# The delta rule of a hybrid trunk: its steps placed by counts of projection matmuls, decays loaded through GpSimd's queue, two buffers for the decayed products

## The chip, the cores and the metric

The kernel runs on one core of a Trainium2 chip. The metric is device time in microseconds (us) of one execution, as the median of three runs. TensorE multiplies (PE in the profile; PEld is its weight load), VectorE (DVE) and ScalarE (ACT) work element by element and empty the accumulation banks, GpSimd (POOL) masks and can issue transfers, SyncE (SP) issues transfers.

## The reference

Two layers, 1024 tokens, width 1024. In each layer one projection of the normalised input gives the inputs of two branches: attention over selected keys, and a gated delta rule with 8 heads of 128 channels. The sum of the two branches, each with its gate, goes through an output projection and is added to the residual. The change concerns the delta rule:

```python
qkv_b = jax.nn.silu(causal_depthwise_conv(qkv_b, conv_w[layer]))
q_b = l2_normalize(q_b...); k_b = l2_normalize(k_b...)
beta = jax.nn.sigmoid(beta_l); g = -jnp.exp(a_log) * jax.nn.softplus(a_l + dt_bias)
# S_t = a_t (I - b_t k_t k_t^T) S_{t-1} + b_t k_t v_t^T,  o_t = S_t^T q_t,  a_t = exp(g_t)
o_b = chunked_gated_delta_rule(q_b, k_b, v_b, beta, g)
y_b = rms_norm(o_b, gdn_norm_gain) * jax.nn.silu(z_b)
```

The chunked form needs, for each head and chunk, the products k·k and q·k times a matrix of decays, the inverse of a unit triangular matrix, and then a loop over the chunks that carries the state.

## The kernel before, in words

Numbers are float32; the large projections split each operand into a high and a low part and add three float32r matmuls (line 361 for the projections whose output has channels on the partitions). The delta rule uses chunks of 128 tokens, 8 per head.

`feature_phase` (L639) runs once per layer and holds all of the delta rule. Per head, `gdn_front` (L672) projects keys, queries and values (`proj_feat`, L354: two halves of 512 tokens, 24 matmuls each), evacuates them on ScalarE (L687, L688), convolves on VectorE (L694) and applies silu (L696, L697). It then transposes keys and queries on TensorE (L708), squares and adds them on ScalarE (L723, 16 squares of 128 columns, each with a read of its sum), scales kdec and vb from the transposes on VectorE (L713), turns the norms into coefficients (L727 to L737), sends one row of them through memory (L739 to L747), multiplies keys with keys and queries (L758) and multiplies the products with the decays H (L760, L761). `inverse_blocks` (L829) takes the diagonal 32x32 blocks of H through memory into the tile "wide", inverts them in 31 pairs of VectorE operations over 8 rows each (L847, L849), and reads them back through memory (16 reads, L855). `inverse_pairs` (L858) joins blocks in two levels with small matmuls (L871 to L892). `gdn_chunks` (L766) walks the chunks: r from the state (L780, L782), u (L784, copied on VectorE, L786), the next state (L789, L794), the output in two matmuls into two halves of a bank (L797, L798) that VectorE combines (L802, L803), and a square on ScalarE (L806). `gdn_finish` (L810) computes the two gate projections of a head, the norm (L817 to L821), transposes the output (L825), multiplies (L826) and writes it out.

`decay_rows` (L660) loads one head's decays, spread to all partitions, on SP's queue, masks them on GpSimd (L666) and exponentiates them on ScalarE (L669); it runs one head ahead, with three buffers H.

In program order a head's front comes before the previous head's finish, and its chunks behind that. The order on each engine is made by the framework's scheduler: it takes what its own model of time says is ready, by program order, and `high_priority(offset=AHEAD)` puts the block inverses first. Each engine then keeps that order on the chip. The accumulators are two banks "acc" and one "more", in turn; transposes and products share two banks "tr"; the chunk loop has two banks "ch" and one "oc".

Of the kernel before, what the change touches and what calls it, by code (L numbers as in the profile page):

```python
# [25 lines left out]
F32 = mybir.dt.float32  # L26
# [4 lines left out]
AF = mybir.ActivationFunctionType  # L31
# [5 lines left out]
P = 128  # L37
# [31 lines left out]
AHEAD, BEHIND = 1000, -10  # L69
# [17 lines left out]
class Trunk:  # L87
    def __init__(self, ctx, tc, args):
# [10 lines left out]
        self.beside = None  # L99
        ctx.enter_context(self.banks(acc=(1, 2), tr=(1, 2)))  # L100
# [49 lines left out]
    def constants(self, first):  # L150
# [25 lines left out]
        for q in range(4):  # L176
            nc.gpsimd.affine_select(self.xinit[32 * q:32 * q + 32], self.xinit[32 * q:32 * q + 32],
                                    pattern=[[1, 8], [-1, 32]], compare_op=OP.not_equal, fill=1.0, base=8 * q,
                                    channel_multiplier=0)
# [113 lines left out]


# [59 lines left out]
    def proj_feat(self, ws, half, act, evac, tag="acc"):  # L354
# [3 lines left out]
        for k in range(KT):  # L358
            cs = slice((k % 4) * P, (k % 4 + 1) * P)
            for i, (a, b) in enumerate(((0, 0), (0, 1), (1, 0))):  # L360
                self.nc.tensor.matmul(acc, ws[k // 4][a][:, cs], act[b][:, k, hs], start=k == 0 and i == 0,  # L361
                                      stop=k == KT - 1 and i == 2)
        evac(hs, acc)
        self.tick()
# [48 lines left out]
    def decays(self, l, p, raw):  # L413
# [41 lines left out]
        row = p.tile([64, P], F32, name="row")  # L455
        nc.vector.tensor_copy(row, pr[:64, :P])
        self.rows = self.dram.tile([T, 8, P], F32, name="rows")
        nc.sync.dma_start(out=self.rows.rearrange("t h c -> (t h) c"), in_=row)
# [159 lines left out]
    def gated(self, l, ht, cz, cg, tag="acc"):  # L618
# [4 lines left out]
        for half in range(2):  # L623
            b = p.tile([P, 512], F32, name="gate", bufs=2)
            for i in range(2):
                def evac(hs, acc):
                    th = p.tile([P, 512], F32, name="th", bufs=2)
                    nc.scalar.activation(th, acc, AF.Tanh, scale=0.5)
# [10 lines left out]
    def feature_phase(self, l, ht):  # L639
        nc, tc = self.nc, self.tc  # L640
        self.yb = self.dram.tile([HEADS, P, S], F32, name="yb")
        with tc.tile_pool(name="feat", bufs=1) as p, self.banks(ch=(1, 2), oc=(1, 1), more=(1, 1)):
            XF = p.tile([P, T, 64], F32, name="xf")
            nc.gpsimd.memset(XF, 0.0)
            heads = {}
            E = self.decay_rows(p, 0)
            for h in range(HEADS + 1):
                if h < HEADS:
                    H, E = E, self.decay_rows(p, h + 1) if h + 1 < HEADS else None
                    heads[h] = self.gdn_front(l, p, ht, h, H)  # L650
# [4 lines left out]
                if h:  # L655
                    self.gdn_finish(l, p, ht, heads.pop(h - 1))
                if h < HEADS:
                    self.gdn_chunks(p, heads[h], XF)

    def decay_rows(self, p, h):  # L660


        nc = self.nc
        E = p.tile([P, T, P], F32, name="H", bufs=3)
        nc.sync.dma_start(out=E, in_=ap(self.rows, h * P, [[0, P], [8 * P, T], [1, P]]))
        nc.gpsimd.affine_select(E, E, pattern=[[0, T], [1, P]], compare_op=OP.is_ge, fill=MASKED, base=0,  # L666
                                channel_multiplier=-1)
        for c in range(T):
            nc.scalar.activation(E[:, c], E[:, c], AF.Exp, bias=self.ngm[:, c, h:h + 1])  # L669
        return E  # L670

    def gdn_front(self, l, p, ht, h, H):  # L672
        nc = self.nc
        w = self.w_in[l]
        feat = self.feat[l]
        kf = p.tile([P, S], F32, name="kf", bufs=3)
        qf = p.tile([P, S], F32, name="qf", bufs=3)
        vv = p.tile([P, S], F32, name="vv", bufs=1)
        for base, dst in ((1024, kf), (0, qf), (2048, vv)):
            ct = (base + h * P) // P  # L680
            cw = lambda j: feat[:, 24 * j + ct:24 * j + ct + 1]
            xp = p.tile([P, S + 4], F32, name="xp", bufs=2)
            nc.gpsimd.memset(xp[:, 0:4], 0.0)

            def evac(hs, acc):
                o = hs.start
                nc.scalar.copy(xp[:, 4 + o:516 + o], acc)  # L687
                nc.scalar.activation(dst[:, hs], acc, AF.Copy, scale=cw(3))  # L688

            ws = self.feat_weights(w, C_QKVB + base + h * P)  # L690
            for half in range(2):
                self.proj_feat(ws, half, ht, evac)
            for j in range(3):
                nc.vector.scalar_tensor_tensor(dst, xp[:, 1 + j:1 + j + S], cw(j), dst, op0=OP.mult, op1=OP.add)  # L694
            th = xp[:, 4:4 + S]
            nc.scalar.activation(th, dst, AF.Tanh, scale=0.5)  # L696
            nc.vector.scalar_tensor_tensor(dst, th, 1.0, dst, op0=OP.add, op1=OP.mult)  # L697

        sm = self.small
        beta, egc, egs = (a[:, :, h] for a in (self.beta, self.egc, self.egs))  # L700
        kdec = p.tile([P, T, P], F32, name="kdec", bufs=2)
        vb = p.tile([P, T, P], F32, name="vb", bufs=2)

        def turn(src, half):
            pt = self.tr()
            for i in range(4):
                c = 4 * half + i
                nc.tensor.transpose(pt[:, i * P:(i + 1) * P], src[:, c * P:(c + 1) * P], self.ident)  # L708
            return pt

        def scaled(dst, pt, col, half):
            cs = slice(4 * half, 4 * half + 4)
            nc.vector.tensor_mul(dst[:, cs], pt.rearrange("p (c d) -> p c d", c=4),  # L713
                                 col[:, cs, None].to_broadcast([P, 4, P]))
# [431 lines left out]
```

## Time and profile before

| | |
|---|---|
| median of 3 runs | 2727.01 us (2726.43 to 2728.11) |
| the profiled execution | 2725.06 us, span 2723.3 us |
| TensorE busy | 2570.7 us, 94% |
| VectorE, ScalarE, GpSimd busy | 1972.8, 1316.8, 111.9 us |
| mean granted TensorE clock | 0.976 of full speed |
| feature phase, layer 0 | 358.0 to 1096.9 us |
| feature phase, layer 1 | 1702.5 to 2452.0 us |

All numbers of one profile belong to one execution. Busy time counts an instruction from its start to its end, and matmuls overlap, so a busy TensorE is not one at its peak. The granted clock is a share of full speed: 1.0 is 2.4 GHz and 0.5 is 1.2 GHz, and a value between is a mean over the stretch. The phases' bounds are the first matmul of the first head's keys and the end of the last output transposes.

### The profile page before, as it was taken

How to read it: one execution, taken by the hardware profiler on the slowest of the kernel's cores; microseconds unless marked ns; L12 is line 12 of the kernel's file. 1: busy time of each engine (PE TensorE's matmuls, PEld its weight loads, DVE VectorE, ACT ScalarE, POOL GpSimd, SP SyncE). 2: the span in 40 equal slices, each digit the busy share in tenths (PEclk: the TensorE clock that was granted, in tenths of full speed). 3: DMA queues.
4: the chain of work that ended last, by engine and by line, in shares of the span. 5: the costliest groups of instructions: out<-in, count | busy, mean ns of one | idle time of the engine just before them, and what ended most of it. 6: DMA issues, size and time to landing. Idle time of an engine off the chain costs nothing.

```text
span 2723.3 us, 42939 instructions
## 1 busy us (share of the span) xinstructions
PE 2570.7 (94%) x14854; PEld 2140.5 (79%) x14854; DVE 1972.8 (72%) x5450; ACT 1316.8 (48%) x3169; POOL 111.9 (4%) x398
## 2 busy tenths in 40 slices
PE   7999989999999999999999999898999999999998
PEld 7677778777777888898786777686887778888986
DVE  6677967767787775697366888677676777757965
ACT  5579643343333332697245894433333343227962
POOL 0122000000000000000001210000000000000000
PEclk9999999999999999999999999998899999999999
DMA  3113332222222221531420232321212221226324
GB/s 121 48 66 90 85 87 56 49 51 57 61 51 53 50 73 51 174 105 35 157 65 30 78 101 71 77 63 47 53 42 65 51 57 46 69 63 180 92 68 143
DMA packets 283262, 202.95 MB, mean 75 GB/s; under 512 B 55906, under 2 KB 241188, under 8 KB 283044
## 3 DMA queue, kind: packets, MB, share of 16 engines
q1 hardware_dynamic: 283044, 200.20, 26.2%
q8 instruction: 117, 1.92, 0.3%
q14 instruction: 101, 0.83, 0.1%
HBM read 153.80 MB, written 46.33 MB: 73 GB/s over the span
## 4 chain that ended last, share of the span: by engine, by line
PE 68%; DVE 13%; ACT 7%; DMA 6%; issue 5%; POOL 1%; SPq 0%; DVEq 0%; POOLq 0%; ACTq 0%
PE acc L361 20%; PE acc L338 11%; PE more L361 9%; PE acc L1038 4%; PE wide L1006 4%; PE tr L758 2%; PE tr L1029 2%; ACT t_junk L562 2%; PE out L338 2%; ACT g_junk L723 2%; DMA w_raw<-in_w_in_dram 2%; DVE t_junk L544 2%; DVE w_lo L140 2%; DMA H<-rows 2%; PE tr L708 1%
## 5 line engine op out<-in xcount | busy, mean ns | idle before, releaser
L361 PE MATMUL acc<-hi_t,w_hi 128*128 128x512 f32 x1240 | 502.2, 405 | 8.3 <-DVE gate L629 7.3
L361 PE MATMUL acc<-hi_t,w_lo 128*128 128x512 f32 x1240 | 501.9, 405 | 0.0
L361 PE MATMUL acc<-lo_t,w_hi 128*128 128x512 f32 x1240 | 499.6, 403 | 0.0
L139 ACT CAST w_hi<-w_raw 128x512 fp32r<-128x512 f32 (+1 forms) x336 | 201.1, 602 | 371.0 <-PE acc L361 196.8
L140 DVE TENSOR_TENSOR w_lo<-w_raw,w_hi 128x512 fp32r<-128x512 f32 (+1 forms) x336 | 223.3, 668 | 149.2 <-ACT w_hi L139 136.0
L338 PE MATMUL acc<-w_hi,hi_t 128*128 128x512 f32 (+1 forms) x768 | 285.7, 373 | 12.6 <-ACT w_hi L139 7.3
L338 PE MATMUL acc<-w_lo,hi_t 128*128 128x512 f32 (+1 forms) x768 | 284.5, 371 | 2.1 <-DVE w_lo L140 1.9
L338 PE MATMUL acc<-w_hi,lo_t 128*128 128x512 f32 (+1 forms) x768 | 283.6, 369 | 0.0
L361 PEld LDWEIGHTS acc<-hi_t,w_hi 128*128 128x128 f32 x1240 | 236.7, 191 | 49.8 <-DVE gate L629 8.6
L361 PEld LDWEIGHTS acc<-hi_t,w_lo 128*128 128x128 f32 x1240 | 236.2, 190 | 41.1
L361 PEld LDWEIGHTS acc<-lo_t,w_hi 128*128 128x128 f32 x1240 | 236.3, 191 | 40.9
L562 ACT ACTIVATE t_junk<-scores,t_bits 128x640 f16<-128x640 f32 x248 | 198.8, 802 | 30.8 <-DVE t_bits L554 26.0
L361 PE MATMUL more<-hi_t,w_hi 128*128 128x512 f32 x488 | 198.8, 407 | 4.5 <-ACT kf L688 4.5
L361 PE MATMUL more<-hi_t,w_lo 128*128 128x512 f32 x488 | 199.2, 408 | 0.0
L361 PE MATMUL more<-lo_t,w_hi 128*128 128x512 f32 x488 | 198.3, 406 | 0.0
L338 PEld LDWEIGHTS acc<-w_hi,hi_t 128*128 128x128 f32 x768 | 146.2, 191 | 40.6 <-ACT w_hi L139 10.5
L338 PEld LDWEIGHTS acc<-w_lo,hi_t 128*128 128x128 f32 x768 | 146.7, 191 | 27.4 <-DVE w_lo L140 5.1
L338 PEld LDWEIGHTS acc<-w_hi,lo_t 128*128 128x128 f32 x768 | 146.6, 191 | 22.0 <-issue 1.0
L544 DVE TENSOR_SCALAR_CACHE_REDUCE t_junk<-scores,t_bits 128x1024 f16<-128x1024 f32 (+4 forms) x136 | 153.4, 1128 | 4.3
L849 DVE TENSOR_TENSOR xc<-xc,xtmp 128x248 f32<-128x248 f32 (+30 forms) x496 | 141.8, 286 | 3.1
L847 DVE TENSOR_TENSOR xtmp<-wide,xc 128x248 f32<-128x248 f32 (+30 forms) x496 | 141.6, 285 | 2.7
L806 ACT ACTIVATE o_junk<-vb 128x128 f32<-128x128 f32 x128 | 39.6, 310 | 162.3 <-DVE vb L803 126.3
(344 smaller groups left out, 5478.4 us busy)
## 6 DMA issues: line engine op xcount, KB each, us to landing
w_raw<-in_w_in_dram SPq DMA_DIRECT2D x272, 256.0 KB
qs<-stage SPq DMA_DIRECT2D x32, 256.0 KB
ya_gate<-gate SPq DMA_DIRECT2D x32, 256.0 KB
H<-rows SPq DMA_DIRECT2D x16, 512.0 KB
wide<-hscr SPq DMA_DIRECT2D x64, 128.0 KB
yb<-gate SPq DMA_DIRECT2D x32, 256.0 KB
w_raw<-in_w_out_dram SPq DMA_DIRECT2D x32, 256.0 KB
qraw<-qs SPq DMA_DIRECT2D x32, 256.0 KB
```

The source lines that it names most:

```text
L139: self.nc.scalar.copy(hi, src)
L140: self.nc.vector.tensor_sub(lo, src, hi.bitcast(F32))
L338: nc.tensor.matmul(acc[t][:, :n], a[:, k, ts], ws[k][b][:, :n], start=k == 0 and i == 0, stop=k == KT - 1 and i == 2)
L361: self.nc.tensor.matmul(acc, ws[k // 4][a][:, cs], act[b][:, k, hs], start=k == 0 and i == 0, stop=k == KT - 1 and i == 2)
L544: nc.vector.tensor_scalar(junk[:, :sc[i].shape[1]], sc[i], thr, 0.0, op0=op, op1=OP.add, accum_out=cnt[:, i:i + 1])
L562: nc.scalar.activation(junk[:, :n], sc[i], AF.Sign, bias=f(bits, i), scale=-1.0, accum_out=cnt[:, i:i + 1])
L723: nc.scalar.activation(junk, pt[:, c * P:(c + 1) * P], AF.Square, accum_out=ssq[:, col:col + 1])
L758: nc.tensor.matmul(pg[:, o0:o0 + P], kf[:, cs], a[:, cs], start=True, stop=True)
L847: nc.vector.tensor_mul(tmp[:, :, j + 1:], ln[:, None, j, j + 1:].to_broadcast(shape), X[:, :, j:j + 1].to_broadcast(shape))
L849: nc.vector.tensor_add(X[:, :, j + 1:], X[:, :, j + 1:], tmp[:, :, j + 1:])
L1006: nc.tensor.matmul(ps[:, :w], qt[a][:, i], kt[b][:, g, o:o + w], start=j == 0, stop=j == 2)
L1038: nc.tensor.matmul(po, a, b[:, cs], start=j == 0 and i == 0, stop=j == t and i == 2)
```

## The change

Every step of a head's delta rule becomes a small function with a position, counted in projection matmuls since the head began. `proj_feat` counts its matmuls; after each it issues the steps that are due, at a priority above everything else, and makes their TensorE instructions follow that matmul and their ScalarE instructions follow the last evacuation. VectorE, SP and GpSimd get no such edge.

```diff
+AT_DECAYS, AT_EXP, AT_KEYS, AT_ROW, AT_QUERIES, AT_PRODUCTS, AT_VALUES, AT_PAIRS, AT_CHUNKS, AT_NORMS, AT_OUTPUTS = (
+    80, 118, (100, 106), 138, (142, 147), (151, 155, 159, 163), (204, 210), 352, 390, 552, (562, 568))
+
+STEP_PAIRS, STEP_CHUNKS = 6, 7
...
+    def planned(self, mm=None):
+        while True:
+            due = [x for x in self.plan if mm is None or x[0] <= self.count]
+            if not due:
+                return
+            first = min(due, key=lambda x: x[:2])
+            self.plan.remove(first)
+            with ExitStack() as ctx:
+                if mm is not None:
+                    ctx.enter_context(self.tc.issue_after(mm))
+                    ctx.enter_context(self.tc.issue_after(self.act_last))
+                ctx.enter_context(self.tc.high_priority(offset=PLANNED))
+                first[2]()
...
+        at(AT_PAIRS, *[lambda: next(pairs, None)] * 6, gap=STEP_PAIRS)
+        chunks = self.gdn_chunks(p, hd)
+        at(AT_CHUNKS, *[lambda: next(chunks, None)] * (3 * T - 1), gap=STEP_CHUNKS)
```

A head's chunks at 390 to 544 thus run during the projections of the next two heads (a head has 240 matmuls in the steady state: 144 for keys, queries and values and 96 for the gates of the head before; the first has 144).

The decays are loaded within the head's own period, through GpSimd's queue, into two buffers instead of three; a second load brings the exponentials of the summed decays, which scale the queries once instead of each chunk's output:

```diff
+        E = hd["H"] = p.tile([P, T, P], F32, name="H", bufs=2)
+        nc.gpsimd.dma_start(out=E, in_=ap(self.rows, h * P, [[0, P], [8 * P, T], [1, P]]))
+        masked = nc.gpsimd.affine_select(E, E, pattern=[[0, T], [1, P]], compare_op=OP.is_ge, fill=MASKED, base=0,
+                                         channel_multiplier=-1)
+        qe = hd["qe"] = p.tile([P, 32, 32], F32, name="wide", bufs=1).rearrange("p a b -> p (a b)")
+        with self.tc.issue_after(masked.ins):
+            nc.gpsimd.dma_start(out=qe.rearrange("p (t c) -> p t c", c=P),
+                                in_=ap(self.rows, (T * 8 + h) * P, [[0, P], [8 * P, T], [1, P]]))
...
+        self.nc.vector.tensor_mul(hd["qf"], hd["qf"], hd["qe"])
```

Work moves between the engines, and some goes:

```diff
+        self.nc.scalar.activation(junk, pt, AF.Square)
+        self.nc.vector.tensor_reduce(ssq, junk.rearrange("p (c d) -> p c d", c=4), axis=AX.X, op=OP.add)
...
+            nc.scalar.activation(hd["vb"][:, c], pt[:, i * P:(i + 1) * P], AF.Copy, scale=hd["br"][:, c:c + 1])
...
-            nc.vector.tensor_copy(u, pu)
+            nc.scalar.copy(u, pu)
...
-                nc.tensor.matmul(po[:, P:2 * P], qf[:, cs], st, start=True, stop=True)
-            nc.tensor.matmul(po[:, :P], A[:, c], u, start=True, stop=True)
-            if st is None:
-                nc.vector.tensor_copy(vb[:, c], po[:, :P])
-            else:
-                nc.vector.tensor_copy(vb[:, c], po[:, :P])
-                nc.vector.scalar_tensor_tensor(vb[:, c], po[:, P:2 * P], egc[:, c:c + 1], vb[:, c], op0=OP.mult,
-                                               op1=OP.add)
+                nc.tensor.matmul(po, qf[:, cs], st, start=True, stop=False)
+            nc.tensor.matmul(po, A[:, c], u, start=st is None, stop=True)
+            nc.scalar.copy(vb[:, c], po)
```

In the block inverse the unit matrix is spread over the partitions so that step j has only j//4+1 rows that are not zero; it goes through memory in 4 writes and 4 reads. The two pairs of the first joining level alternate, block by block, in one bank:

```diff
-            shape = [P, 8, 31 - j]
+            n = j // 4 + 1
+            shape = [P, n, 31 - j]
...
-        for b in (0, 2):
-            k, m = slice(32 * b, 32 * b + 32), slice(32 * b + 32, 32 * b + 64)
-            py = self.bank("ch")
-            for c in range(T):
+        py = self.bank("ch")
+        for c in range(T):
+            for k, m in pairs:
                 nc.tensor.matmul(py[m, 32 * c:32 * c + 32], H[k, c, m], XF[k, c, 0:32], start=True, stop=True)
```

`decays` writes a second set of rows (one matmul and one exponential more per layer), and the two tiles xp are set up once per layer, with their leading zeros, instead of once per projection.

## Rows read from the trace of the kernel before

**Rows 1.** The page: span, and part 1, TensorE's busy time.
```profile
span 2723.3 us, 42939 instructions
...
PE 2570.7 (94%) x14854; PEld 2140.5 (79%) x14854; DVE 1972.8 (72%) x5450; ACT 1316.8 (48%) x3169; POOL 111.9 (4%) x398
```

**Rows 2.** Busy time by stretch, the two feature phases (columns in the first line).
```profile
core 0: us, PE busy (x) PEld busy (x) DVE busy (x) ACT busy (x) POOL busy (x), PEclk, DMA share, GB/s
358.00:1096.90 738.90, 696.44 (x4216) 573.57 (x4216) 528.04 (x1476) 260.68 (x746) 11.58 (x33) 0.97 0.23 58
1702.50:2452.00 749.50, 703.54 (x4220) 582.01 (x4219) 528.42 (x1478) 261.33 (x746) 11.51 (x33) 0.96 0.23 57
```

**Rows 3.** Waits of TensorE: us in total, times, longest us.
```profile
PE tr L825 <- DVE vb L821: 47.9, 10, 6.4
PE tr L708 <- DVE kdec L713: 15.5, 4, 7.3
...
PE more L361 <- ACT kf L688: 4.5, 2, 3.4
```

**Rows 4.** Busy time by stretch, slices of 5 us (columns as in rows 2).
```profile
400.00:405.00 5.00, 0.00 (x0) 0.00 (x0) 3.67 (x4) 4.52 (x19) 0.00 (x0) 0.79 0.49 119
...
620.00:625.00 5.00, 0.47 (x4) 0.42 (x4) 4.95 (x16) 0.95 (x2) 0.10 (x1) 0.98 0.41 105
625.00:630.00 5.00, 5.00 (x24) 4.37 (x23) 3.46 (x10) 1.44 (x8) 0.00 (x0) 0.68 0.43 136
...
2235.00:2240.00 5.00, 3.86 (x17) 3.43 (x18) 3.55 (x10) 0.95 (x3) 0.00 (x0) 0.66 0.18 68
```

**Rows 5.** Timeline of TensorE: start us, us, instruction.
```profile
346.74 0.39 PE L361 MATMUL acc<-hi_t,w_lo 128*128 128x512 f32 x1
346.97 0.39 PE L361 MATMUL acc<-hi_t,w_hi 128*128 128x512 f32 x1
...
417.31 0.49 PE L758 MATMUL tr<-kf 128*128 128x128 f32 x2
...
419.24 0.38 PE L758 MATMUL tr<-kf 128*128 128x128 f32 x2
```

**Rows 6.** Timeline of VectorE: inverse step, r of two chunks, norms of a head.
```profile
504.65 0.39 DVE L847 TENSOR_TENSOR xtmp<-wide,xc 128x232 f32<-128x232 f32 x1
505.10 0.35 DVE L782 SCALAR_TENSOR_TENSOR g_r<-ch,g_nce,vb 128x128 f32<-128x128 f32 x1
...
510.15 0.34 DVE L782 SCALAR_TENSOR_TENSOR g_r<-ch,g_nce,vb 128x128 f32<-128x128 f32 x1
...
537.47 0.17 DVE L817 TENSOR_TENSOR g_ms<-g_osq,g_rq 128x8 f32<-128x8 f32 x1
...
540.30 1.22 DVE L821 TENSOR_TENSOR vb<-vb,rs_y 128x1024 f32<-128x1024 f32 x1
```

**Rows 7.** Costliest groups of VectorE: busy us, mean ns, idle before and its releaser.
```profile
L803 DVE SCALAR_TENSOR_TENSOR vb<-oc,egc,vb 128x128 f32<-128x128 f32 x112 | 38.7, 346 | 1.0
L786 DVE COPY g_u<-ch 128x128 f32<-128x128 f32 x128 | 36.8, 287 | 53.4 <-PE ch L784 53.0
...
L713 DVE TENSOR_TENSOR vb<-tr,g_br 128x512 f32<-128x512 f32 x32 | 21.4, 684 | 5.8 <-PE tr L708 5.4
```

**Rows 8.** The view of line 472: duration in ns, least, median and most.
```profile
L472 DVE TENSOR_REDUCE k_ssq<-relu x2: 678/680/683, 57.9 to 1404.4; 128x8 f32<-128x512 f32 x2
```

**Rows 9.** Costliest groups of ScalarE (columns as in rows 7).
```profile
L723 ACT ACTIVATE g_junk<-tr 128x128 f32<-128x128 f32 x256 | 71.1, 278 | 54.3 <-PE tr L708 47.6
L723 ACT ACTIVATION_READ_ACCUMULATOR g_junk<-tr 128x1 f32 x256 | 50.3, 197 | 0.0
...
L1108 ACT ACTIVATE sq_junk<-x 128x512 f32<-128x512 f32 x16 | 10.0, 625 | 38.1 <-DVE x L1095 31.1 <-DMA x<-th 7.1
```

**Rows 10.** The chain that ended last, 600 to 640 us: start us, us, what.
```profile
599.61 8.24 DMA H<-rows
608.04 1.10 POOL H L666
```

**Rows 11.** Costliest groups of TensorE, line L877 (columns as in rows 7).
```profile
L877 PE MATMUL ch<-H,y 32*32 32x32 f32 x512 | 22.7, 195 | 0.0
```

More of the change, by code (lines that the diff above doesn't have):

```diff
@@ L360, in proj_feat @@
             for i, (a, b) in enumerate(((0, 0), (0, 1), (1, 0))):
[L361 to L362 removed]
+                mm = self.nc.tensor.matmul(acc, ws[k // 4][a][:, cs], act[b][:, k, hs], start=k == 0 and i == 0,
+                                           stop=k == KT - 1 and i == 2)
+                self.count += 1
+                if not (k == KT - 1 and i == 2):
+                    self.planned(mm.ins)
         evac(hs, acc)
+        self.planned(mm.ins)
         self.tick()
@@ L454, in decays @@
         nc.tensor.matmul(pr[:64, :P], g2, self.tri_mid, start=True, stop=True)
[L455 to L458, printed above, removed]
+        nc.tensor.matmul(pr[:64, P:2 * P], g2, self.tri_in, start=True, stop=True)
+        row = p.tile([64, 2, P], F32, name="row")
+        nc.vector.tensor_copy(row[:, 0], pr[:64, :P])
+        nc.scalar.activation(row[:, 1], pr[:64, P:2 * P], AF.Exp)
+        self.rows = self.dram.tile([2, T, 8, P], F32, name="rows")
+        nc.sync.dma_start(out=self.rows.rearrange("a t h c -> (t h) a c"), in_=row)
     def index_scores(self, l, p, raw, scores):
@@ L762, in gdn_front, with gdn_queries @@
-        with self.tc.high_priority(offset=AHEAD):
-            self.inverse_blocks(p, H, ccomp)
-        return dict(h=h, H=H, nc=nc_, kf=kf, qf=qf, kdec=kdec, vb=vb, A=A, nce=nce, rq=rq, rq2=rq2)
-    def gdn_chunks(self, p, hd, XF):
+    def gdn_queries(self, hd, half):
+        self.squares(self.turned(hd["qf"], half), hd["ssq"][:, 8 + 4 * half:12 + 4 * half])
+        if half == 1:
+            zq = hd["zq"] = self.small.tile([P, T], F32, name="g_zq")
+            self.nc.vector.tensor_scalar(zq, hd["ssq"][:, 8:16], 4 * EPS, P * EPS, op0=OP.add, op1=OP.mult)
@@ new lines, in gdn_products @@
+    def gdn_products(self, p, hd, c):
+        nc = self.nc
+        kf, H = hd["kf"], hd["H"]
+        if c == 0:
+            hd["A"] = p.tile([P, T, P], F32, name="A", bufs=2)
+        pg = self.tr()
+        for i in range(2):
+            cs = slice((c + i) * P, (c + i + 1) * P)
+            for j, a in enumerate((kf, hd["qf"])):
+                o0 = 256 * i + P * j
+                nc.tensor.matmul(pg[:, o0:o0 + P], kf[:, cs], a[:, cs], start=True, stop=True)
+        pg4 = pg.rearrange("p (c a i) -> p c a i", c=2, a=2)
+        nc.vector.tensor_mul(hd["A"][:, c:c + 2], pg4[:, :, 1], H[:, c:c + 2])
+        nc.vector.tensor_mul(H[:, c:c + 2], pg4[:, :, 0], H[:, c:c + 2])
@@ L823, in gdn_finish, with norms, outputs @@
+        def norms():
+            o = hd["vb"]
+            ms = self.small.tile([P, T], F32, name="g_ms")
+            nc.vector.scalar_tensor_tensor(ms, hd["osq"], 1.0 / P, hd["zq"], op0=OP.mult, op1=OP.add)
+            rs = self.rsqrt(ms, T)
+            nc.vector.tensor_mul(o, o, rs[:, :, None].to_broadcast([P, T, P]))
+        def outputs(half):
+            h, b = hd["h"], gates[half]
             pt = self.tr()
             for i in range(4):
-                nc.tensor.transpose(pt[:, i * P:(i + 1) * P], o[:, 4 * half + i], self.ident)
+                nc.tensor.transpose(pt[:, i * P:(i + 1) * P], hd["vb"][:, 4 * half + i], self.ident)
@@ L826, in gdn_finish @@
             nc.vector.scalar_tensor_tensor(b, pt, feat[:, 96:97], b, op0=OP.mult, op1=OP.mult)
             nc.sync.dma_start(out=self.yb[h, :, 512 * half:512 * half + 512], in_=b)
+        self.at(hd["at"] + AT_NORMS, norms)
+        for half in range(2):
+            self.at(max(hd["at"] + AT_OUTPUTS[half], self.count + 2), lambda half=half: outputs(half))
     def inverse_blocks(self, p, H, ccomp):
```

256 lines of the change are left out of this document (131 added, 125 removed).

## The prediction

> **What bounds the kernel now.** The page comes first. TensorE is busy for 94% of a span of 2723.3 us [rows 1]; "busy" counts each matmul until it has drained, so the most that a new order can give is TensorE's idle time and the time in which its clock is low. Then the two stretches in which the delta rule runs, one per layer. They last 738.9 and 749.5 us; TensorE is busy for 696.44 and 703.54 of them, at a mean granted clock of 0.97 and 0.96 [rows 2]. So 42.5 + 46.0 = 88.4 us of idle time lie there. VectorE is busy for 528 us in each (71%), ScalarE for 261 (35%), GpSimd for 12.
>
> TensorE's waits say for whom: 47.9 us in ten waits of the output transposes (L825) for the normalised vb (L821), 15.5 us of the query transposes (L708) for kdec [rows 3]. They sit where one head ends and the next begins: the last norm, the transposes of keys and queries and the row of coefficients come close behind each other, and TensorE stands in its order while VectorE catches up. A second price follows such a wait. Between 620 and 625 us TensorE is busy for 0.47 of 5 us; in the next 5 us it is busy throughout, at a clock of 0.68 [rows 4]. For each slice of 5 us I multiplied busy time by the missing clock: 27 slices are below full clock, the first at 400 and the last at 2235 [rows 4], and give 12.4 us in layer 0 and 21.0 in layer 1, together 33.4. The Trainium skill (TensorE: Matmul & The Clock Gate, Part 1) says that the clock falls to 1.2 GHz when the engine has been idle and comes back after sustained work. By that rule the slices of low clock go with the idle time, and the trace agrees: they stand beside idle slices.
>
> **The change, part by part.** Every step of a head gets a position counted in projection matmuls and is issued, ahead of all else, once TensorE has done that many. Such matmuls start 0.23 us apart (0.227 over many) [rows 5]. A head has 240 of them in the steady state, 54 us; a gap of 7 is 1.6 us.
>
> *The head's boundary* (the term that decides). Each step has its own place: keys 100, row 138, queries 142, products 151 to 163, and projection matmuls lie between. I take off the 88.4 us of idle without the 4.5 us in which TensorE waits for ScalarE's first copies of kf [rows 3], which the change does not touch: 83.9. With the idle stretches nothing is left that lowers the clock: 33.4. Each of the 33 waits in these stretches also hides 0.16 us as "busy" (a matmul drains for 0.39 us where the next would start after 0.23 [rows 5]): 5. Bounds: nothing, if the waits come back elsewhere; or 122.3, and with the mean clocks of rows 2 instead of my slices, 0.03 x 696 + 0.04 x 704 = 49 us, another 15.6. I take the slices, which show where TensorE worked.
>
> *What is left of it.* Norms stand at 552, the transposes of the outputs at 562. The norms take 14 small operations in 2.8 us now and a product of 1.22 (537.47 to 541.5) [rows 6]; 12 small ones and the product make 3.65, and the plan leaves 10 x 0.227 = 2.27. The scheduler may move the transposes back by itself; now it does so well enough in 6 of 16 heads (ten waits). So 1.4 us in ten heads: 14, between 0 and 22.
>
> *The products.* Their four steps start 1.93 us apart now (417.31, 419.24) [rows 5], held by VectorE, two multiplications each among its other work; the plan gives 4 x 0.227 + 0.89 = 1.8. With two banks the last two wait 0.25 us each: 8 us in 16 heads, between 0 and 16.
>
> *VectorE's work per head.* Taken away: 7 combinations of vb at 0.346 us, 8 copies of u at 0.287, 8 copies to vb that I price the same, 2 scalings of vb at 0.684 [rows 7]: 8.4 us. The 62 steps of the inverse touch 1560 elements a partition instead of 3968, twice; 232 elements take 0.39 us [rows 6], a small operation 0.17, so 1 ns an element: 4.8 us. Added: four reductions at 0.68 [rows 8] and one product over 1024 at 1.22, 3.9 us. Net 9 us less of 66. It lies beside TensorE's work and is counted at nothing; it is what lets the plan hold, and if VectorE were the bound it would be worth 9 x 16 = 144.
>
> *ScalarE's work per head.* Added: 24 copies and scalings of 128 columns at 0.28, 6.7 us, and four squares of 512 at 0.63, 2.5. Taken away: 16 squares at 0.278 with 16 reads at 0.197 [rows 9], 7.6. Net 1.6 us on an engine that idles for 65%: nothing; without that cover 1.6 x 16 = 26.
>
> *The queues.* SP loses the load of H and 12 of 16 reads of the inverse and gains 3 writes per head. Weight loads stand behind them, and no wait of TensorE in the two stretches is for one: nothing either way. GpSimd loses the memsets of xp and gets H, its mask, and behind the mask the new 512 KB of query decays, due only at 163. H takes 8.24 us to land and 1.10 to mask now [rows 10]. Between positions 80 and 118 lie 38 x 0.227 = 8.6 us and 3 us of transposes: 11.7 against 9.3. No row has a transfer issued by GpSimd: it lands between as now and far later. I take as now, the same bytes into the same tile. What waits behind it is the mask on GpSimd and the eight exponentials on ScalarE, with the copies out of the accumulators behind these. With two buffers for H instead of three, the load for head k+2 follows the last chunk of head k by 16 matmuls in the steady state. Head 2 alone is 80 matmuls late (head 0 has a period of 144), 18 us; between 0 and 2 x 15; I take 0, since its pairs come over 130 matmuls after H is then there.
>
> *TensorE's own work* stays, but for one matmul a layer. The two block pairs now alternate in one bank; by the forms as they run they cost the same. If alternate blocks ran side by side, half of the 45 us of L871 and L877 (22.7 each, [rows 11]) would go: 0 to 23. The Trainium skill (TensorEngine Tiling (Array Packing), Key Properties) lets tiles work independently, which would give the 23; its Restrictions and Gotchas forbid row tiles to use one bank at the same time, which gives 0. I take 0: no row shows blocks side by side.
>
> **Sum.** The profiled execution took 2725.06 us (span 2723.3). 2725.1 - 122.3 + 14 + 8 = 2624.8. The median stands 1.9 above that execution: 2627 us.
>
> **Rivals.** (1) *The steps' own trips become the bound: slower.* 23 chunk steps and 6 pair steps per head are issued 7 or 6 matmuls after the one before: 29 x 16 = 464 places where TensorE, in order, stands if the operation between is late. A chunk takes 5.05 us now where VectorE is full (505.10, 510.15) [rows 6]; the plan gives 21 x 0.227 + 1.0 = 5.8. It decides from a mean lateness of 100 / 464 = 0.22 us per step; at 0.35 it costs 162: 2789. For it: an operation of 1.2 us can stand ahead of a step. Against: VectorE loses 9 us a head, and one trip of three in a chunk leaves it. (2) *Half of the boundary returns* as waits at the two transpose banks, because VectorE is late where keys, queries, products and inverse gather: half of 122.3, 2688. For it: a position orders TensorE and ScalarE, not VectorE. Against: the steps have 10 us between groups. (3) *H comes late through GpSimd.* If it landed 5 us later, ScalarE would stand some 3 us before its exponentials in each of 16 heads, and TensorE behind full accumulators: 48 us, 2675. The Trainium skill (DMA: Bandwidth & Descriptors, SWDGE vs HWDGE vs iDMA) says that GpSimd writes its descriptors into SBUF, where VectorE can lock it out in some modes, and that the hardware queues never meet that; no run here shows it. (4) *The plan does not bite:* the holes stay where they are, 2727.
>
> **How the numbers follow.** Forecast 0.64, rival 1 0.09, rival 2 0.14, rival 3 0.10, rival 4 0.03. A measurement of this kernel can tell about 0.2% (5.5 us) from no change. Forecast and rivals 2 and 3 are faster: 0.88; rival 4 is the same: 0.03; rival 1 is slower: 0.09. Low end: 2627 less 22 (nothing left at outputs and products), 15.6 (clock) and 23 (pairs): 2566. High end: rivals 2 and 3 with ScalarE's 26 on top of the smaller: 2701, say 2700; rivals 1 and 4 stay outside.
>
> **What would show it.** Right: the two stretches last about 690 us; L708 has nearly no wait and L825 less than a third; the clock is 1.00 in nearly all slices; VectorE's busy time falls by some 70 us in each and ScalarE's rises by 10 to 15. Rival 1: many waits under 1 us of the chunk's matmuls for g_r, u or g_s. Rival 2: waits of several us at transposes or products. Rival 3: ScalarE idle before the exponentials for GpSimd or for H, copies behind it. I am wrong if TensorE is still idle for over 40 us in the two stretches together, or if that is gone and they still last over 715 us each: then small matmuls between large ones cost more than I see.

## The result, and the profile after

The changed kernel takes 2749.22 us, the median of 7 runs (2738.21 to 2758.32), against 2728.11 for the kernel before beside it: a ratio of 1.008, 95% interval 1.0059 to 1.01. It is slower by 0.8%, where 2627 us was forecast. The kernel of before, run again beside each experiment, took 2725.79 to 2727.74 us, so medians of different runs can be set side by side to about 3 us. The profiled execution of the changed kernel took 2755.04 us. Of the changed kernel: the page; TensorE's waits; and busy time by stretch, the two feature phases and slices of 5 us at two of these waits (columns as in [rows 2]):

```profile
span 2753.4 us, 42170 instructions
...
PE 2595.2 (94%) x14858; PEld 2134.8 (78%) x14858; DVE 1886.2 (69%) x5082; ACT 1348.4 (49%) x3107; POOL 135.4 (5%) x386
```
```profile
PE tr L909 <- DVE vb L903: 48.2, 12, 6.7
PE tr L765 <- issue: 18.0, 2, 9.0
...
PE ch L965 <- DVE xf L956: 10.7, 4, 4.8
PE tr L831 <- DVE H L834: 10.2, 2, 5.2
```
```profile
359.50:1122.30 762.80, 711.86 (x4219) 578.51 (x4220) 485.80 (x1293) 275.93 (x712) 23.59 (x27) 0.96 0.32 66
1734.00:2478.00 744.00, 701.79 (x4220) 571.70 (x4219) 486.32 (x1296) 277.00 (x715) 23.43 (x27) 0.97 0.30 68
...
390.00:395.00 5.00, 0.00 (x0) 0.00 (x0) 4.20 (x4) 0.00 (x0) 0.73 (x3) 0.80 0.81 68
395.00:400.00 5.00, 1.08 (x5) 1.11 (x6) 4.96 (x5) 2.15 (x3) 0.00 (x0) 0.50 0.22 53
400.00:405.00 5.00, 5.00 (x19) 4.10 (x18) 4.34 (x10) 2.80 (x5) 0.00 (x0) 0.67 0.00 0
...
695.00:700.00 5.00, 0.29 (x2) 0.00 (x0) 1.38 (x5) 0.00 (x0) 1.65 (x2) 1.00 0.20 31
700.00:705.00 5.00, 3.42 (x12) 3.09 (x13) 3.56 (x6) 0.00 (x0) 0.30 (x1) 0.52 0.72 75
```

TensorE idles for 762.80 - 711.86 = 50.9 us in the first phase and 42.2 in the second: 93.1, against 88.4 before [rows 2]. The missing clock (busy time times the share of the clock that is not granted), summed over slices of 5 us as in the prediction, is 23.0 + 12.0 = 35.0 us, against 33.4. So the idle time that was to go is all there, and the output transposes (L825 before, L909 now) wait for the norms as long as before [rows 3]. No wait for kdec is left. New are 9 us of waiting at the transposes of head 0 in each layer and the waits for H; those for xf are 10.7 us in 4, where one of 4.5 us stood before. The first phase is longer by 23.9 us, the second shorter by 5.5; 1.5 + 6.1 + 4.1 us come on top ahead of, between and behind the phases. Over the whole span TensorE's busy time is up by 24.5 us ([rows 1] and the page above) and its idle time by 5.6.

The timeline shows where the six us of a head's end come from. Of the changed kernel, around 690 us, VectorE, SyncE (SPq), GpSimd and TensorE in turn:

```profile
692.36 0.43 DVE L956 STREAM_TRANSPOSE xf<-H 32x256 f32<-32x256 f32 x1
692.82 0.17 DVE L140 TENSOR_TENSOR rs_t<-rs_y 128x8 f32<-128x8 f32 x1
698.48 0.44 DVE L956 STREAM_TRANSPOSE xf<-H 32x256 f32<-32x256 f32 x1 [5.50 <-DMA H<-xscr]
...
700.30 1.22 DVE L903 TENSOR_TENSOR vb<-vb,rs_y 128x1024 f32<-128x1024 f32 x1
```
```profile
683.42 2.51 SPq L944 DMA_DIRECT2D xscr<-xc  x4
...
687.38 1.83 SPq L947 DMA_DIRECT2D H<-xscr  x4
```
```profile
687.53 0.89 POOL L722 DMA_DIRECT2D H<-rows  x1 [60.18 <-ACT g_u L872]
698.35 1.09 POOL L723 TENSOR_SCALAR_AFFINE_SELECT H<-H 128x1024 f32<-128x1024 f32 x1 [9.93 <-DMA H<-rows]
```
```profile
701.58 1.97 PE L909 MATMUL tr<-ident,vb 128*128 128x128 f32 x8 [6.28 <-DVE vb L903]
```

VectorE is in the middle of one head's norms (L140). Between their small operations stand the three transposes (L956) that begin the next head's block pairs. The third waits 5.50 us for the return from memory of that head's inverse, 128 KB issued at 687.38; everything behind it on VectorE waits too, the norms among it, and TensorE waits 6.28 us for these. The return is late while another transfer is under way: at 687.53 GpSimd, whose buffer for H has just come free, issues the 512 KB of the following head's decays, and both land within 0.2 us of each other, at about 698.4. So it goes at eight of the 16 heads: GpSimd issues the load of H 2.0 to 4.1 us after the write of the inverse, and L909 waits 4.9 to 6.7 us, 47.2 of its 48.2 in all. At the other eight no load of H is under way during the inverse's trip, and L909 waits for the norms 0.3 us at most.

The waits for xf have the same source, with the other new load. At heads 0 and 2 of either layer the load of the queries' decays is issued beside the write of the inverse (SyncE, then GpSimd, of the changed kernel, head 0):

```profile
470.32 2.58 SPq L944 DMA_DIRECT2D xscr<-xc  x4
...
481.69 1.81 SPq L947 DMA_DIRECT2D H<-xscr  x4
```
```profile
470.38 0.91 POOL L727 DMA_DIRECT2D wide<-rows  x1 [79.64 <-DVE xc L940]
```

At these four heads the return is issued 11.4, 8.9, 8.3 and 6.7 us after the write, and the four waits of L965 stand there. At eleven of the other twelve it is issued 3.9 to 4.3 us after it; at the last, one of the eight, H's load already meets the write, and it is 11.6.

At head 0 there is one more chain (VectorE, then GpSimd, of the changed kernel):

```profile
390.77 2.60 DVE L755 SCALAR_TENSOR_TENSOR kf<-xp,feat,kf 128x1024 f32<-128x1024 f32 x2 [9.30 <-POOL xp L682]
```
```profile
389.56 1.09 POOL L723 TENSOR_SCALAR_AFFINE_SELECT H<-H 128x1024 f32<-128x1024 f32 x1 [2.46 <-DMA H<-rows]
390.61 0.13 POOL L682 MEMSET xp<- 128x4 f32 x2
```

The first convolution waits 9.30 us for the zeroing of four columns of xp, 0.13 us of work. On GpSimd it stands behind the masking of two heads' H, each of which waits for its load.

### The profile page after: what moved, and what is told of

It reads as the page before. It is cut to its first block, busy times and chain, and to the rows that moved or that the text cites. A ratio compares the mean times of both kernels' runs of the same rounds, so it can differ in the third digit from the quotient of the medians.

```text
span 2753.4 us, 42170 instructions
## 1 busy us (share of the span) xinstructions
PE 2595.2 (94%) x14858; PEld 2134.8 (78%) x14858; DVE 1886.2 (69%) x5082; ACT 1348.4 (49%) x3107; POOL 135.4 (5%) x386
## 4 chain that ended last, share of the span: by engine, by line
PE 56%; DVE 11%; DMA 7%; issue 3%; ACT 2%; SPq 1%; POOL 0%; DVEq 0%; ACTq 0%; POOLq 0%
PE acc L388 16%; PE more L388 7%; PE acc L365 7%; PE acc L1137 4%; PE wide L1105 4%; PE tr L1128 2%; DMA H<-xscr 2%; PE out L365 2%; DVE xtmp L938 2%; DVE xc L940 2%; PE tr L831 2%; PE out L388 2%; PE tr L765 1%; DVE w_lo L148 1%; DMA wide<-rows 1%
## 5 line engine op out<-in xcount | busy, mean ns | idle before, releaser
L388 PE MATMUL acc<-lo_t,w_hi 128*128 128x512 f32 x1240 | 511.4, 412 | 0.0
L388 PE MATMUL acc<-hi_t,w_hi 128*128 128x512 f32 x1240 | 503.2, 406 | 6.8 <-DVE gate L663 6.1
L388 PE MATMUL acc<-hi_t,w_lo 128*128 128x512 f32 x1240 | 503.7, 406 | 0.0
L365 PE MATMUL acc<-w_hi,hi_t 128*128 128x512 f32 (+1 forms) x768 | 287.5, 375 | 15.1 <-ACT w_hi L147 10.2
L365 PE MATMUL acc<-w_lo,hi_t 128*128 128x512 f32 (+1 forms) x768 | 286.8, 374 | 2.1 <-DVE w_lo L148 2.1
L365 PE MATMUL acc<-w_hi,lo_t 128*128 128x512 f32 (+1 forms) x768 | 285.2, 371 | 0.0
L388 PEld LDWEIGHTS acc<-hi_t,w_hi 128*128 128x128 f32 x1240 | 236.3, 191 | 57.2 <-DVE gate L663 7.5
L388 PEld LDWEIGHTS acc<-lo_t,w_hi 128*128 128x128 f32 x1240 | 236.8, 191 | 47.7
L388 PEld LDWEIGHTS acc<-hi_t,w_lo 128*128 128x128 f32 x1240 | 236.8, 191 | 45.3
L388 PE MATMUL more<-lo_t,w_hi 128*128 128x512 f32 x488 | 203.0, 416 | 0.0
L388 PE MATMUL more<-hi_t,w_hi 128*128 128x512 f32 x488 | 199.7, 409 | 1.7 <-ACT kf L749 1.7
L388 PE MATMUL more<-hi_t,w_lo 128*128 128x512 f32 x488 | 198.9, 408 | 0.0
L365 PEld LDWEIGHTS acc<-w_hi,hi_t 128*128 128x128 f32 x768 | 146.8, 192 | 45.6 <-ACT w_hi L147 13.9
L365 PEld LDWEIGHTS acc<-w_lo,hi_t 128*128 128x128 f32 x768 | 147.4, 192 | 28.5 <-DVE w_lo L148 5.3
L365 PEld LDWEIGHTS acc<-w_hi,lo_t 128*128 128x128 f32 x768 | 147.4, 192 | 22.8 <-issue 1.0
L886 ACT COPY vb<-oc 128x128 f32<-128x128 f32 x128 | 34.1, 267 | 178.1 <-PE oc L885 169.8
L940 DVE TENSOR_TENSOR xc<-xc,xtmp 128x60 f32<-128x60 f32 (+24 forms) x496 | 104.9, 212 | 12.5
L938 DVE TENSOR_TENSOR xtmp<-wide,xc 128x60 f32<-128x60 f32 (+24 forms) x496 | 103.9, 210 | 12.4
```

The costliest lines, as they stand in the source:

```text
L365: nc.tensor.matmul(acc[t][:, :n], a[:, k, ts], ws[k][b][:, :n], start=k == 0 and i == 0, stop=k == KT - 1 and i == 2)
L388: mm = self.nc.tensor.matmul(acc, ws[k // 4][a][:, cs], act[b][:, k, hs], start=k == 0 and i == 0, stop=k == KT - 1 and i == 2)
L938: nc.vector.tensor_mul(tmp[:, :n, j + 1:], ln[:, None, j, j + 1:].to_broadcast(shape), X[:, :n, j:j + 1].to_broadcast(shape))
L940: nc.vector.tensor_add(X[:, :n, j + 1:], X[:, :n, j + 1:], tmp[:, :n, j + 1:])
```

## The experiments

**The place of the weights in SBUF.** One more difference fits the slowdown: matmuls of the projections start 0.2267 us apart before the change and 0.2333 after it, also where the plan is not active (300.19 to 313.79 us against 300.14 to 314.14, 60 steps each). The change makes the pool of small tiles smaller by 192 bytes a partition, so that the weights' pool behind it lies at 94080 instead of 94272 (bytes in a partition, by the layout of the kernel's pools; no trace prints them). An unused tile moves it:

```diff
+        self.pad = self.small.tile([P, 48], F32, name="pad", bufs=1)
+        self.nc.gpsimd.memset(self.pad, 0.0)
```

> The changed kernel with one unused tile of 192 bytes, so that the pool of weights and gates lies at 94272 again, as before the change (the change had moved it to 94080). Nothing that the kernel computes, waits for or issues is touched. Theory A (the place of the weights in SBUF sets the spacing of the projections' matmuls): spacing of back-to-back 128x512 matmuls falls from 0.2333 to 0.2267 us, 5376 times 0.0066 us or 35 us are gained, and about 2712 us result, with the waits as they were. Rival B (the spacing comes from the plan, its semaphores or the chip): spacing stays 0.233 and the time stays at 2749 within 6 us.

2749.44 us (2735.52 to 2751.95), ratio 1.0073, 1.0055 to 1.0091: no change clear of the spread. But the spacing is 0.2267. Half of A holds, and its price does not.

> The kernel of before with one unused tile of 64 bytes, so that the pool of weights lies at 94336 instead of 94272: the same remainder by 128 as after the change, with no plan. Theory A: spacing rises from 0.2267 to about 0.2333 us and the time from 2728 to about 2763 us. Rival B: spacing 0.2267, time 2728. Between them: if only the distance of the weights from the activations or another remainder counts, the spacing may come out at some third value, or stay.

(The same tile with 16 elements.) 2738.74 us, ratio 1.0049, 1.0037 to 1.0061, spacing 0.2333. The place sets the spacing; it costs 12 us here and not 35: in the profiled execution TensorE's busy time rises by 26.4 us against [rows 1] and its idle time falls by 7.5. Why the changed kernel gained nothing, one place shows: one wait of TensorE for the gate and the slice of 5 us behind it, timeline and busy time, first of the changed kernel, then of the run with the pool moved back:

```profile
332.81 0.40 PE L388 MATMUL acc<-hi_t,w_lo 128*128 128x512 f32 x1
335.74 0.50 PE L388 MATMUL acc<-hi_t,w_hi 128*128 128x512 f32 x1 [2.54 <-DVE gate L663]
```
```profile
335.00:340.00 5.00, 4.26 (x18) 3.47 (x19) 3.55 (x7) 0.00 (x0) 0.00 (x0) 1.00 0.56 144
```
```profile
330.01 0.39 PE L390 MATMUL acc<-hi_t,w_lo 128*128 128x512 f32 x1
334.04 0.50 PE L390 MATMUL acc<-hi_t,w_hi 128*128 128x512 f32 x1 [3.63 <-DVE gate L665]
```
```profile
335.00:340.00 5.00, 5.00 (x17) 3.95 (x16) 3.69 (x4) 0.00 (x0) 0.00 (x0) 0.70 0.54 143
```

The faster matmuls reach the same late gate sooner, wait 1.1 us longer, and then run at a clock of 0.70 where the slower ones keep 1.00. Here the wait and the clock take back what the spacing gives. Over the whole span, in slices of 5 us, TensorE is busy for 17.0 us less with the pool moved back, idles for 160.2 us instead of 158.2, and misses 51.2 us of clock instead of 45.8. But that profiled execution, 2740.09 us, lies 9 us below the median of its kernel, so it is not shown in full how the two medians come out alike.

**The order on VectorE.** The first step of the block pairs held behind the previous head's outputs:

```diff
-            nc.vector.transpose(XF[bs, :, co:co + 32], XT[bs, :, bs])
+            with ExitStack() as ctx:
+                if self.out_last is not None and hd["h"]:
+                    ctx.enter_context(self.tc.issue_after(self.out_last))
+                nc.vector.transpose(XF[bs, :, co:co + 32], XT[bs, :, bs])
```

(`out_last` is the last multiplication of `outputs`.)

> The changed kernel with the pairs' first step (three transposes on VectorE) held behind the last VectorE instruction of the previous head's outputs. Theory C (the outputs' transposes on TensorE wait 6 us a head because the norms stand on VectorE behind a transpose that waits for the DMA of the inverse): the wait of L909 for the norms, 48.2 us in 12, falls below 8 us, and the time by 35 to 55 us (the low clock behind the stalls included), to about 2700 us. Rival D (the stall only moves: the transposes are as late, and the pairs' matmuls wait instead): the waits of L965 rise from 10.7 us to over 40 us and the time stays within 10 us of 2749.

2697.47 us, ratio 0.989, 0.9875 to 0.9904. Its waits of TensorE (the line numbers have moved by one to four):

```profile
PE tr L766 <- issue: 19.3, 2, 9.9
...
PE ch L969 <- DVE xf L960: 10.6, 4, 5.1
PE tr L832 <- DVE H L835: 9.8, 2, 5.0
...
PE tr L910 <- DVE vb L904: 3.1, 10, 0.5
```

Theory C: 48.2 us became 3.1, the waits for xf stay, and 52 us are gained.

**The load beside the return.** Three buffers for H, the load behind the previous head's values, and the load of the queries' decays behind the return; a GpSimd copy of one element that reads the tile in question holds each back:

```diff
-        at(AT_DECAYS, lambda: self.decays_load(p, hd))
+        at(AT_DECAYS - 120 if hd["h"] > 1 else AT_DECAYS, lambda: self.decays_load(p, hd))
+        at(AT_DECAYS, lambda: self.decays_queries(p, hd))
...
-        E = hd["H"] = p.tile([P, T, P], F32, name="H", bufs=2)
+        E = hd["H"] = p.tile([P, T, P], F32, name="H", bufs=3)
+        if h > 1:
+            mark = self.small.tile([1, 16], F32, name="mark")
+            late = nc.gpsimd.tensor_copy(mark[:, 0:1], hd["prev"]["vb"][0:1, T - 1, 0:1])
...
+            after = nc.gpsimd.tensor_copy(mark[:, 0:1], hd["prev"]["H"][96:97, T - 1, 96:97]).ins
+        with self.tc.issue_after(after):
```

> The changed kernel with three buffers for H and the load of H a good half period earlier (behind the previous head's values), and the load of the queries' decays behind the return of the inverse; the order on VectorE is as in the changed kernel. Theory E (the inverse's return is late because the 512 KB load of H is in flight beside it): the third transpose L956 no longer waits 5.5 us for the return, the wait of L909 for the norms falls from 48.2 us to below 15 us, the wait of the products for H of head 2 (10.2 us) goes, and the time falls by 40 to 65 us, to about 2695 us. Rival (the round trip through memory takes its 10 us alone): L956 still waits about 5 us a head, and the time falls by some 10 us at most.

2662.16 us, ratio 0.9764, 0.9751 to 0.9776: 87 us less than the changed kernel, above what was expected. Its SyncE and GpSimd around one return:

```profile
660.28 2.51 SPq L959 DMA_DIRECT2D xscr<-xc  x4
...
664.23 1.83 SPq L962 DMA_DIRECT2D H<-xscr  x4
```
```profile
668.83 0.31 POOL L740 COPY mark<-H 1x1 f32<-1x1 f32 x1 [18.42 <-DMA H<-xscr]
```

The copy of one element runs when the return has landed, 4.6 us after its issue; it was 11.1 in the changed kernel (687.38 to 698.48). Over all heads that have the copy it is 3.3 to 4.6 us; at seven of the eight heads that stall in the changed kernel the transpose starts 7.7 to 11.1 us after the issue, and at the eighth the write was late instead. The waits of the output transposes (L909 in the changed kernel) fall from 48.2 us to 7.5, those for xf and for H of head 2 are gone.

To see whether the bytes did it, and not the buffers or the queue, a transfer of the same size, from the same rows into memory that nobody reads, was added alone, as soon as the inverse is done:

```diff
+        done = nc.gpsimd.tensor_copy(mark[:, 0:1], self.xc[0:1, 7, 31:32])
+        extra = self.dram.tile([P, T, P], F32, name="extra", bufs=2)
+        with self.tc.issue_after(done.ins):
+            nc.gpsimd.dma_start(out=extra, in_=ap(self.rows, h * P, [[0, P], [8 * P, T], [1, P]]))
```

> The run with H early alone (2662 us, the inverse's return landed 4.6 us after its issue), with the suspected cost put back and nothing else: beside each return GpSimd issues a transfer of 512 KB from the same rows into memory that nobody reads, as soon as the inverse is done. Theory E (the bytes in flight delay the return): the third transpose on VectorE waits 4 to 6 us for the return again, the outputs' transposes on TensorE 4 to 6 us a head behind it, and the time rises by 40 to 60 us, to about 2710. Rival (it was the place of H's load in the queue or its two buffers, not the bytes): the time stays at 2662 within 8 us.

2784.33 us, ratio 1.0216, 1.0192 to 1.024: 122 us more, twice what was expected. Its SyncE, GpSimd, and TensorE's waits:

```profile
692.17 2.52 SPq L970 DMA_DIRECT2D xscr<-xc  x4
...
703.12 2.49 SPq L973 DMA_DIRECT2D H<-xscr  x4
```
```profile
692.33 0.78 POOL L742 DMA_DIRECT2D extra<-rows  x1
707.11 0.28 POOL L751 COPY mark<-H 1x1 f32<-1x1 f32 x1 [14.00 <-DMA H<-xscr]
```
```profile
PE tr L935 <- DVE vb L929: 57.5, 12, 7.9
PE ch L991 <- DVE xf L982: 36.2, 6, 7.5
```

Placed that early the transfer meets the write of the inverse and not its return: the return is issued 10.95 us after the write (703.12 - 692.17) instead of 3.95, and lands 4.0 us after its issue, no later than the 4.6 without the transfer. The whole trip takes 14.9 us instead of 8.6. So it is at all 14 heads that have the added transfer, 10.9 to 12.5 us from write to return; at the last head of each layer, which has none, it is 4.0 and 3.9. Theory E is shown for the trip as a whole: 512 KB of another queue in flight make it some 6 us longer. That a load beside the return alone holds it up rests on the seven heads of the changed kernel against the run with H early; other sizes were not tried. The Trainium skill (DMA: Bandwidth & Descriptors, Queues, rings and completion order) says that each DMA engine takes packets from the queues that have work in turn; the longer trip agrees with that, but no view here shows the packets one by one.

**The zeroing on GpSimd.**

```diff
-                nc.gpsimd.memset(a[:, 0:4], 0.0)
+                nc.vector.memset(a[:, 0:4], 0.0)
```

> The changed kernel with the zeroing of the two convolution buffers' margins (four columns each, once a layer) on VectorE instead of GpSimd. Theory F (TensorE stands 9.0 us at head 0 of either layer because the first convolution waits for that zeroing, which stands on GpSimd behind the masking of H, which waits for H's load): the wait of L765 named issue, 18.0 us in 2, falls below 3 us, VectorE's wait for xp (18.5 us in 2) goes, and the time falls by 15 to 25 us, to about 2730 us. Rival: something else of head 0 is as late (H, the keys' convolution itself), and TensorE stands there 5 us or more a layer still; the time falls by less than 8 us.

2724.98 us, median of ten runs (2721.08 to 2742.18), ratio 1.0011, 0.9991 to 1.003. The waits named issue at head 0 fall from 18.0 us to 1.4, the others stay as they were (L909 49.8 us in 12). That is theory F, worth 24 us by the medians, though the ten runs spread over 21.

**The three together.**

> The changed kernel with all three edits: the transposes of the pairs held behind the previous head's outputs, H in three buffers and loaded early, the zeroing on VectorE. The weights' pool lies at 94208, as in the run with H loaded early alone. If the three waits are what is left of the sum of the prediction, the idle time of TensorE in the two feature phases falls to about 10 us, and the time from 2662 to 2635 us within 8. If the order on VectorE matters only beside the late return, the order edit adds nothing here (below 4 us), and 2643 us result from the zeroing alone.

2637.18 us (2636.1 to 2638.09), ratio 0.9673, 0.9657 to 0.9688. Its feature phases and its longest waits in them:

```profile
358.20:1057.30 699.10, 688.61 (x4219) 563.26 (x4219) 488.57 (x1296) 276.38 (x715) 28.51 (x38) 1.00 0.34 72
...
1664.90:2363.20 698.30, 687.99 (x4221) 564.33 (x4220) 488.68 (x1296) 276.62 (x715) 28.50 (x38) 1.00 0.32 72
```
```profile
PE acc L389 <- DVE gate L664: 8.5, 4, 3.2
...
PE tr L925 <- DVE vb L919: 5.5, 12, 0.6
PE tr L818 <- DVE g_nc L809: 5.1, 4, 2.2
```

TensorE idles for 10.5 + 10.3 = 20.8 us, where about 10 was expected, and the missing clock is 6.8. This kernel beats both: 89 us less than before, 112 less than the changed one.

> H early and the zeroing on VectorE, without the edge on VectorE's order: the run with all three edits less the order. If the order matters only beside a late return, 2637 us as with all three, within 4 us. If the order is worth something of its own, 2645 us or more.

2642.61 us, ratio 0.9687, 0.9672 to 0.9701. Between the two expectations: the order gives 5 us by the medians, but the intervals of the two ratios overlap. Of the 52 us that it gave alone, nearly all came from keeping the late return away from the norms.

> The same added transfer in the run with all three edits (2637 us). If the order on VectorE is what turns a late return into a stall, the transposes that wait for it now stand behind the outputs, and the time rises by less than 15 us. If a late return stalls TensorE whatever the order (the pairs' matmuls come next), it rises by 30 us or more.

2714.01 us, ratio 0.9941, 0.9917 to 0.9964: 77 us more. Two of its waits of TensorE:

```profile
PE ch L995 <- DVE xf L986: 33.7, 6, 6.9
...
PE tr L936 <- DVE vb L930: 5.6, 12, 0.6
```

The order takes away the norms' share of the stall: 57.5 us in 12 beside the same transfer without the order, 5.6 with it. The pairs' waits for xf are not that share moved, for the run without the order has them too, 36.2 us in 6; in both they stand at heads 0 to 2 of either layer. So a late return costs TensorE in two ways, and the order stops one. With these waits comes the clock: over the whole span idle time is 121.8 us instead of 80.1, the missing clock 54.2 instead of 12.4.

> The run with the three edits and one unused tile of 64 bytes more, so that the weights' pool lies at 94272 as before the change. The place set the matmuls' spacing (0.2267 us there, 0.2289 to 0.2334 at the three others) but not the time of the changed kernel, whose stalls took up the gain. Theory: without the stalls the spacing shows in the time; at 0.2267 us for 7680 matmuls, by 0.002 to 0.007 us each, 15 to 40 us less than the run without the tile, less what the granted clock gives back. Rival: the time is the same within 5 us, because the denser matmuls lose as much to the low clock.

2641.82 us, ratio 0.9694, 0.9673 to 0.9714, spacing 0.2267 (0.2288 without the tile, 300.05 to 313.78 in 60 steps): no gain, as the rival had it. The phases last 699.3 and 699.6 us, and the stretch behind them, with the clock at 0.98 instead of 0.99, 277.7 instead of 271.0. Over the whole span TensorE idles for 89.3 us instead of 80.1, and 27.9 us of clock are missing instead of 12.4.

**One part alone on the kernel of before.** Only the shorter inverse and its return in four transfers:

> The kernel of before with only the change's inverse: the steps on as many rows as are filled, and the return in four transfers of 32 rows. VectorE has about 8 us less to do in each head. Theory G (before the change the outputs' transposes wait 5 to 6 us a head for norms behind a full VectorE): the wait of L825, 47.9 us in 10, falls by more than half and the time by 25 to 50 us. Rival (the same wait is there for the order of VectorE's work, whatever its amount): the wait stays above 35 us and the time within 10 us of 2727.

2709.91 us, median of ten (2694.73 to 2722.83), ratio 0.9935, 0.9911 to 0.9959. Of its waits:

```profile
PE ch L874 <- DVE xf L867: 20.8, 8, 5.5
...
PE tr L825 <- DVE vb L821: 3.6, 6, 1.5
```

The waits of L825 fall from 47.9 us to 3.6, and before the change VectorE is busy for 4.95 of 5 us beside such a wait (620 to 625 us, [rows 4]): G names the cause of the stall before the change. The edit also makes 4 transfers of the return out of 16, and no run tries that by itself. The gain is smaller than expected. TensorE's idle time in the phases falls from 88.4 to 53.2 us, but its busy time there rises by 14.1 for the same matmuls, with 53.4 us of clock missing instead of 33.4: what is left of the waits still comes in pieces of up to 5.5 us. The phases are 21.1 us shorter together, the span of the profiled execution 15.7.

**The block pairs.**

```diff
-        for c in range(T):
-            for k, m in pairs:
+        for k, m in pairs:
+            for c in range(T):
```

> The run with all three edits (2637 us), with the two block pairs of the first level one behind the other again, as before the change, in place of alternating; same bank, same matmuls. Theory H (matmuls of alternate blocks run side by side on the array, which the prediction bounded at 23 us and took at nothing): a group of 32 takes about 1.4 us instead of 0.69, and with TensorE nearly always busy the time rises by 32 times 0.7 us, to about 2659. Rival (the shorter busy time is only how overlapping records are drawn): the time stays at 2637 within 5 us.

2645.36 us, ratio 0.9708, 0.9695 to 0.9721. TensorE's timeline, alternating and one behind the other:

```profile
669.95 0.69 PE L984 MATMUL ch<-xf,H 32*32 32x32 f32 x32
...
674.37 0.69 PE L998 MATMUL ch<-y,H 32*32 32x32 f32 x16
```
```profile
672.85 1.09 PE L984 MATMUL ch<-xf,H 32*32 32x32 f32 x32
```

A float32 matmul of the code stands in the timeline twice, so 32 are 16 of the code. Alternating, 32 take as long as 16 of one block; serial, they take 1.09. In the trace the alternating ones start in pairs, 6 to 7 ns apart, a pair about every 32 ns, where one block alone starts one about every 32 ns. So they run side by side, and it shows in the time: 8 us, less than the 22 expected; by the group, 32 x 0.4 = 13 were to be had.

## Why the prediction was wrong

**The step that failed** is the term that decided, the head's boundary: "Each step has its own place", so the idle time goes. I had its other case as a bound ("nothing, if the waits come back elsewhere") and gave rival 2 half of it, with the right reason, that a position does not order VectorE. I did not follow that reason to an instruction: the pairs' first step has no matmul and no ScalarE work, so nothing held it to its place, and it landed among the norms. I priced none of what stands on VectorE behind the wait for the return. Held to its place by one edge, it lets the output transposes wait 3.1 us instead of 48.2, and 52 us are gained: in place of "the idle time goes", 93.1 us of it stood.

**The queues** were where the cost came from. I priced the move of H to GpSimd by when H lands, and that price was nearly right: a median of 9.3 us in the changed kernel, against 8.24 [rows 10]. I did not ask what is in flight beside it. With two buffers the load for head k+2 starts when head k ends its chunks, and that is when the inverse of head k+1 is on its way through memory: the change made them meet, at eight heads of 16. The second load, the queries' decays, I asked only when it is due; at heads 0 and 2 it met the write of the inverse. Rival 3 had the right transfer and the wrong victim. And I wrote that GpSimd loses the memsets of xp; it keeps two per layer, and I did not look at what they stand behind.

**The size of it.** From 2749 to the forecast 2627 are 122 us. In steps, by the medians: the two loads moved away from the inverse's trip, with the third buffer, 87, the zeroing 20 (2662 to 2643), the order 5; 10 are left. H of head 2, taken at 0 between 0 and 30, cost 10.2 us in two waits.

**What held** is the sum itself, once these are out, and in part by luck: the block pairs gave about 8 us that the sum had at nothing. With the three edits idle time falls by 88.4 - 20.8 = 67.6 us where I had 83.9 - 22 = 61.9, and the missing clock by 26.6 where I had 33.4. The outputs wait 5.5 us instead of 14, and no wait of the products is left. The phases last 699 us, "about 690" was forecast. ScalarE's busy time rose by 15 us a phase in the changed kernel, as worked out; VectorE's fell by 42, not 70; the sum had counted it at nothing, and why it fell short was not looked for. Rival 1 did not happen: with the three edits the chunk's matmuls wait for g_r 1.6 us in all, in 6, and the changed kernel's list has no such wait; the slower side came by a mechanism that I had not named.

**The pairs**, taken at 0 between 0 and 23: the two groups are busy for 25.7 us alternating and 37.1 serial, worth 8. The Trainium skill (TensorEngine Tiling (Array Packing), Restrictions and Gotchas), which I had set against this gain, says that row tiles cannot use one PSUM bank at the same time; here both blocks of a group write one bank, on partitions 32 to 63 and 96 to 127, and 32 take the 0.69 us of 16. The measurement decides.

**My own test of being wrong** was idle time over 40 us in the phases together: 93.1.

## What to carry to other kernels

When a load moves to another queue or loses a buffer, ask when it will now start and which small round trip is in flight then, not only when it lands: 512 KB beside a trip of 128 KB to memory and back stalled VectorE, and TensorE behind it, while the load itself landed about as forecast. An order planned for two engines must be followed through the third: look for the step that has no instruction on the planned ones, and for single small instructions (a memset) behind a wait on a queue that used to be empty. And where a part only shortens waits without removing them, the clock can take back a part: when the inverse alone was shortened, 35 us of idle time went and 14 us of busy time came for the same matmuls.

## What the runs showed of the hardware

The place of the weights in SBUF sets how far apart the large matmuls start. At 94272 both kinds of projection have 0.227 us from one matmul to the next. At 94080 and 94336 those whose output has channels on the partitions (L388 in the changed kernel) have 0.2333 and the others (L365) 0.229 to 0.230; at 94208 it is the other way round. It was worth 12 us in one of three kernels and nothing clear of the spread in the other two, where idle time and missing clock rose in the denser run. Which property of the address decides was not tried.

Beside a transfer of 512 KB from another queue, the trip of 128 KB through memory and back took 14.9 us instead of 8.6; there the write was held up. With the transfer beside the return it took 15.1 us (683.42 to 698.48 in the changed kernel).

Matmuls of two 32x32 blocks on different rows and columns of the array, alternating in one bank, run side by side: 0.69 us for 32 instead of 1.09.
